# A fourth unscaled gate tile, a transposed copy of the S5 output, a column form of the last norm, and pools that wait tile by tile

## The chip, the cores and the metric

The kernel runs on one core of a Trainium2 chip. The metric is the device time of one execution in microseconds (us), as the median of three runs. The engines are named as in the profile: PE is TensorE's matmul, PEld its weight load, DVE is VectorE, ACT is ScalarE, POOL is GpSimd, and SP is the queue that issues most of the DMAs.

## What is computed

One layer of a hybrid decoder for T = 1056 tokens: 1024 of a prompt and 8 sequences of 4 sampled tokens, D = 1024 channels, all in float32.

```
h      = rmsnorm(x, g_mix)
q,k,v,u,gates = split(h @ w_in)            # 1024 | 256 | 256 | 1024 | 2048 columns
a_out  = attention(q, k, v) @ w_attn_o     # window 128, 16 heads, sinks
y      = S5(u)                             # diagonal state space, 64 groups of 16 channels
glu    = gelu(y) @ w_glu
s_out  = glu[:, :1024] * sigmoid(glu[:, 1024:])
x      = x + (sigmoid(gates[:, :1024])*a_out + sigmoid(gates[:, 1024:])*s_out) @ w_out
x      = x + square(relu(rmsnorm(x, g_ffn) @ w_up)) @ w_down
out    = rmsnorm(x, g_final)
```

The new keys and values and the S5 states are returned too.

## The kernel before, in words

Channels lie on the 128 partitions and tokens along the free dimension, so x is 8 tiles of 128 by 1056. A product in float32 is made of three matmuls on rounded halves (lines 117 to 119): weights and activations are each split into a high part (a cast on ACT) and a low part (a subtraction on DVE). A weight block is loaded by SP into `raw`, cast at line 91 and subtracted at line 92; `raw`, `whi` and `wlo` have two buffers each. An output tile of 128 columns of weights takes three chunks of 352 tokens, with 8 times 3 matmuls each, and three PSUM banks (`mm`) for the chunks.

**The start.** `start` (line 166) loads the 8 tiles of x, and makes `hh` (line 181, ACT) and `hl` (line 182, DVE). The same function squares each x on ACT (line 186) and adds the squares into `acc` on POOL (line 188, seven additions of 128 by 1056). `first_tiles` multiplies the first two gate tiles, g0 and g1, with k outermost: each k of them needs only that `hh[k]` and `hl[k]` are there. `token_norms` (line 191) then turns `acc` into the norm factor of each token with small matmuls (line 198), a square root with one Newton step (`rsqrt_newton`, line 155), and spreads the factors over the partitions with matmuls against the identity (line 207) into `rb`. The first `RAW` gate tiles are stored without that factor; it is multiplied in much later, ahead of the sigmoid.

**The order of the tiles.** `cols_in` (line 97) lists the 26 tiles of w_in that come ahead of k and q: g0 g1 g2 u0 u1 u2, then u, g and g+5 in turn, the last gates, and v0, v1. `tile_in` takes the next of the list. A u tile is scaled and transposed into the buffer `Up` by DVE (`u_evac`, line 430), and `Up` (one buffer) goes to DRAM. S5 parameters (`s5_params`, some 150 DVE operations on 64 or 32 columns) and tables (`s5_tables`, with two multiplications on POOL, lines 391 and 402) are made meanwhile. In the loop over m (line 697 on), each of the eight S5 blocks is `s5_x` (matmuls of line 649, then a chain over ACT and DVE up to `HB`, lines 651 to 670) and `s5_y` (matmuls of line 680 that read `HB`, then GELU, then a store to `ydram`). Tiles are put between the two by hand, so that PE has work while the chain runs: one tile and `s5_b` where m is in `SKIP`, two otherwise.

**The middle.** After the S5 part come the two k tiles, the q tiles, and attention, in which a generator (`filler`) hands matmuls of q and of the GLU to PE between the attention blocks. `glu_input` (line 977) loads a tile of `ydram`, whose tokens lie in S5 order (token within block, block), and brings it to token order while it splits it: ACT at line 985, DVE at line 986, each in one piece of 1024 columns with a stride and one of 32. The first GLU tile has k outermost and needs each k as it comes.

**The end.** `last_down` (line 1492) adds the last part of w_down in three token chunks: 512, 288 and 256 tokens. For each of the 8 output tiles DVE adds (line 1543), ACT squares and scales (1545, 1546), and the squares are summed (line 1548: on POOL in the first chunk, on DVE in the others). While a chunk runs, `finish` normalizes the one before: one matmul with a matrix of ones gives each partition all the token sums (line 1497), Newton's square root runs on 128 by 512 or 128 by 288 elements (lines 157 to 162), and 8 multiplications (line 1506: all on POOL for the first chunk, half of them for the second) give the output, which SP stores. The last chunk is finished by rows (`finish_rows`).

**Queues and pools.** Each engine works its instructions off in one order, which is not that of the code: the trace shows DVE running parameter operations of line 276 on ahead of `hl` of later k. Memory comes from pools that are opened and closed; a pool opened over memory of a closed one is by default held until all that used the old pool is done. Line numbers here and in the rows are those of the kernel before.

Of the kernel before, what the change touches and what calls it, by code (L numbers as in the profile page):

```python
# [45 lines left out]
def hybrid_kernel(tc, xt, cache_k, cache_v, h0, norms, w_in, sinks, w_attn_o, lam_re, lam_im, log_dt,  # L46
# [17 lines left out]
    def bank(pool=None):  # L64
        return new(psax, [P, 512], F32, "ax")
# [19 lines left out]
    def wblock(w, n, nk=KT, pool=wts):  # L85

        raw = new(wts, [P, KT, P], F32, "raw")
        nc.sync.dma_start(raw[:, :nk], w[n])
        hi = new(pool, [P, KT, P], F32R, "whi")
        lo = new(pool, [P, KT, P], F32R, "wlo")  # L90
        nc.scalar.copy(hi[:, :nk], raw[:, :nk])  # L91
        nc.vector.tensor_tensor(lo[:, :nk], raw[:, :nk], hi[:, :nk].bitcast(F32), op=ALU.subtract)  # L92
        return hi, lo


    CB = {"u": 12, "g": 20, "v": 10}
    cols_in = [("g", 0), ("g", 1), ("g", 2), ("u", 0), ("u", 1), ("u", 2)]
    cols_in += [t for i in range(3, 8) for t in (("u", i), ("g", i), ("g", i + 5))]
    cols_in += [("g", i) for i in (13, 14, 15)] + [("v", 0), ("v", 1)]
    loaded = []  # L100

# [8 lines left out]
    def gemm(*args, **kw):  # L110
        for _ in gemm_steps(*args, **kw):
            pass
# [48 lines left out]
        nc.vector.tensor_scalar(tmp2, tmp2, -0.5, 1.5, op0=ALU.mult, op1=ALU.add)  # L161
        nc.vector.tensor_tensor(out, tmp1, tmp2, op=ALU.mult)

    RAW = 3

    def start(st, small_loads):

        nc.scalar.dma_start(gcol, norms)
        acc = new(st, [P, T], F32, "acc")
        xs = []  # L170
        for k in range(KT):
            x = new(st, [P, T], F32, "x", 8)
            nc.sync.dma_start(x, xt[k])
            if k in (0, PF2):
                prefetch(wts if k else st)
            if k == PF3:
                prefetch()
            if k == SLK:
                small_loads()
            g = gcol[:, 0, k:k + 1]  # L180
            nc.scalar.activation(hh[k], x, AF.Copy, scale=g)
            nc.vector.scalar_tensor_tensor(hl[k], x, g, hh[k].bitcast(F32), op0=ALU.mult, op1=ALU.subtract)  # L182
            xs.append(x)
        for k, x in enumerate(xs):
            sq = new(st, [P, T], F32, "sq", 3) if k else acc
            nc.scalar.activation(sq, x, AF.Square)
            if k:
                (nc.vector if k in AV else nc.gpsimd).tensor_tensor(acc, acc, sq, op=ALU.add)
        return acc

    def token_norms(st, acc):
# [17 lines left out]
            nc.scalar.copy(rb[:, 3 * c * P:3 * c * P + w], ps[:, :w])  # L209

    PF3 = 5
    AV, PF2, SLK = (), 1, 1


    AR0, AI0, R8 = 0, 9, 18
# [169 lines left out]
    def s5_tables(Y, Ys, fr, fi):  # L385
        nc.scalar.activation(XC[64:128], XC[64:128], AF.Copy, scale=-1.0)
        nc.scalar.activation(Ys[0:64], Ys[0:64], AF.Copy, scale=-1.0)

        sh = [P, G, CH]
        nc.vector.tensor_tensor(BB, Y, fr[:, :, None].to_broadcast(sh), op=ALU.mult)  # L390
        nc.gpsimd.tensor_tensor(Ys, Ys, fi[:, :, None].to_broadcast(sh), op=ALU.mult)
        nc.vector.tensor_tensor(BB, BB, Ys, op=ALU.add)

        H0s = new(slabA, [P, 4, SB, 16], F32, "slab")
        swap(H0s, H0, s0=-1.0)
        sh = [P, 4, SB, 16]

        def pw(col):
            return TP[:, col].rearrange("p (q g) -> p q g", q=4)[:, :, None, :].to_broadcast(sh)

        nc.vector.tensor_tensor(FS, H0, pw(AR0 + 4), op=ALU.mult)
        nc.gpsimd.tensor_tensor(H0s, H0s, pw(AI0 + 4), op=ALU.mult)
        nc.vector.tensor_tensor(FS, FS, H0s, op=ALU.add)
    def s5_phases(TE):

# [113 lines left out]


    S5Q = nc.sync
    NT0 = 4
    with tc.tile_pool(name="ptmp", bufs=1) as pt:
        with tc.tile_pool(name="start", bufs=1) as st:
            prm = []
# [6 lines left out]
            tile_in()  # L532
        s5_tables(Y, Ys, *ft[:2])

    s5w = s5c.enter_context(tc.tile_pool(name="s5work", bufs=1))

    def s5_a(m):

# [187 lines left out]


    mid = es.enter_context(ExitStack())
    qpool = mid.enter_context(tc.tile_pool(name="qpool", bufs=4))
    gen = mid.enter_context(tc.tile_pool(name="gen", bufs=4))  # L730
    late = mid.enter_context(tc.tile_pool(name="late", bufs=1))
    WIN = 128
    kpool = es.enter_context(ExitStack())
    kp = kpool.enter_context(tc.tile_pool(name="kpool", bufs=2))
    kk = [new(kp, [P, T], F32, "kk") for _ in range(2)]

    def scaled_evac(dst, s=None):
        def ev(n, cs, ps):
            if s is None:
                nc.vector.tensor_tensor(dst[:, cs], ps, rb[:, cs], op=ALU.mult)  # L740
            else:
                nc.vector.scalar_tensor_tensor(dst[:, cs], ps, s, rb[:, cs], op0=ALU.mult, op1=ALU.mult)
        return ev

    for i in range(2):
        gemm(wblock(w_in, KT + i), hh, hl, 8, scaled_evac(kk[i]))
    for i in range(2):
        nc.gpsimd.dma_start(k_prompt[i], kk[i][:, SEQ - WIN:SEQ])

# [225 lines left out]
    sdram = [new(dram, [P, T], F32, f"sd{m}") for m in range(KT)]  # L975

    def glu_input(k):
        yt = new(gen, [P, TC, NY], F32, "slab")
        nc.sync.dma_start(yt, ydram[k])
        h = new(slabA, [P, T], F32R, "slab")  # L980
        l = new(slabA, [P, T], F32R, "slab")
        for o, i, pat in ((slice(0, SEQ), yt[:, :, 0:NK], "p (k j) -> p j k"),
                          (slice(SEQ, T), yt[:, 0:ST, NK:NY], "p (b j) -> p j b")):
            hv = h[:, o].rearrange(pat, j=i.shape[1])
            nc.scalar.copy(hv, i)
            nc.vector.tensor_tensor(l[:, o].rearrange(pat, j=i.shape[1]), i, hv.bitcast(F32), op=ALU.subtract)
        gh.append(h)
        gl.append(l)

# [35 lines left out]
        for _ in range(n):  # L1025
            next(fill, None)

    with tc.tile_pool(name="attn", bufs=1) as atp:
        prev = turned = None
        for m in range(2):  # L1030
            for _ in q_proj(m):
                pass
        units = [(kv, blk) for kv in range(NKV) for blk in range(NB)]
        qs = split_q(0, 0)
        kh = new(atp, [P, SEQ], F32R, "kh")
        kl = new(atp, [P, SEQ], F32R, "kl")
        key_stack(0, 0)
        for u, (kv, blk) in enumerate(units):
            if blk == 0:
                key_stack(kv, 1)  # L1040
            if blk == KAHEAD and kv + 1 < NKV:
                key_stack(kv + 1, 0)
            qs, qn = (split_q(*units[u + 1]) if u + 1 < len(units) else None), qs
            cur = (kv, blk) + attend_p(kv, blk, qn, kh, kl)
            more(MORE[u][0])
            if turned is not None:
                attend_v(*turned)
            turned = attend_t(*prev) if prev is not None else None
            more(MORE[u][1])
            prev = cur  # L1050
        attend_v(*turned)
        turned = attend_t(*prev)
        more(2)
        attend_v(*turned)
    with tc.tile_pool(name="sattn", bufs=1) as sp:
        qd = [new(sp, [P, SB, ST, NH], F32, "qd", 2) for _ in range(2)]
        smask = new(sp, [NR, NKEY], F32, "smask")
        vn4 = new(sp, [ST, SB, NKV * HD], F32, "vn4")
        sample_queries()
        prev = None  # L1060
        for g in range(SB // GB):
            if g % 2 == 0:
                load_cache(g // 2)
            cur = sample_p(g)
            more(SMORE[0])
            if prev is not None:
                sample_v(*prev)
            prev = cur
            more(SMORE[1])
        sample_v(*prev)  # L1070
# [421 lines left out]
    def last_down(ws, fh, fl):  # L1492

        def finish(c0, cw, acc):

            ps = bank()
            nc.tensor.matmul(ps[:, :cw], ones, acc[:, :cw], start=True, stop=True)
            ms = new(slabA, [P, 2, 512], F32, "slab")
            r = new(const, [P, T], F32, "rb")[:, :cw]
            nc.vector.tensor_scalar(ms[:, 0, :cw], ps[:, :cw], 1.0 / D, EPS, op0=ALU.mult, op1=ALU.add)  # L1500
            rsqrt_newton(r, ms[:, 0, :cw], acc[:, :cw], ms[:, 1, :cw])
            yield
            for m in range(KT):
                yo = new(slabB, [P, 512], F32, "slab")[:, :cw]
                e = nc.gpsimd if m in YP[c0 > 0] else nc.vector
                e.tensor_tensor(yo, x2[m][:, c0:c0 + cw], r, op=ALU.mult)
                o = min(c0, 512)
                nc.sync.dma_start(y_cols[m, :, o:o + cw], yo)
                yield

        def finish_rows(c0, tiles, acc, banks):

# [8 lines left out]
            for i, (t0, w) in enumerate(tiles):  # L1521
# [2 lines left out]
                nc.scalar.activation(yo[:, 512:], banks[i][1], AF.Copy, scale=r[:, i:i + 1])  # L1524
                for h, eng in enumerate((nc.sync, nc.scalar)):
                    eng.dma_start(y_rows[t0 - c0:t0 - c0 + w, h * 512:h * 512 + 512], yo[:, h * 512:h * 512 + 512])

        YP = (range(8), (1, 3, 5, 7))

        def turn(pss, k, t0, w):  # L1530
            nc.tensor.transpose(pss[k // 4][:w, (k % 4) * P:(k % 4 + 1) * P], x2[k][:, t0:t0 + w], ident)
# [119 lines left out]
```

## Time and profile before

| | us |
|---|---|
| runs (median of 3, lowest to highest) | 1719.57 (1718.57 to 1720.12) |
| the profiled execution, its own time | 1723.68 |
| its span, first to last instruction | 1720.6 |
| PE busy | 1652.6 (96%) |
| DVE busy | 1254.6 (73%) |
| ACT busy | 865.1 (50%) |
| POOL busy | 288.6 (17%) |
| mean granted PE clock | 0.982 of full speed |

The span is measured between instructions; some 3.1 us of the execution lie outside it. A granted clock of 1.0 is 2.4 GHz, 0.5 is 1.2 GHz. Busy times of PE overlap between neighbours, since matmuls are pipelined; what one of them takes is read from the distance of their starts.

### The profile page before, as it was taken

To read this page: it belongs to the slowest core of one execution; us is meant where nothing else is said; L and a number is where in the kernel's file an instruction comes from. 1 tells how busy PE (TensorE), PEld (TensorE's weight loads), DVE (VectorE), ACT (ScalarE), POOL (GpSimd) and SP (SyncE) were. 2 spreads that over 40 slices of the span, in tenths; PEclk is the share of its full clock that TensorE was granted. 3 is DMA by queue.
4 is the path that set the end of the run, shared out by engine and by line. 5 is a ranking of instruction groups with operands and counts; after the bars stand their busy time and mean duration, and the time that the engine had idled before them with its cause. 6 is when DMAs were issued, how large, how long until landed. Compare 5 with 4: busy or idle time off the path is not lost. (4 is left out here: it accounts for less than half of the span.)

```text
span 1720.6 us, 30881 instructions
## 1 busy us (share of the span) xinstructions
PE 1652.6 (96%) x11952; PEld 1618.7 (94%) x11952; DVE 1254.6 (73%) x2449; ACT 865.1 (50%) x1878; POOL 288.6 (17%) x250
## 2 busy tenths in 40 slices
PE   6989999999999899989999999999999999999997
PEld 5979999999999799979999999999999999999986
DVE  8888787744488999952543677777777788787857
ACT  5344444332267888854432555444444645454454
POOL 5211111101133443521122330000000000000014
PEclk8989999999999999999999999999999999999999
DMA  5144433443110321133343563444444665353322
GB/s 208 63 151 139 136 98 121 139 122 112 53 38 26 102 89 50 63 100 111 117 136 126 185 193 113 145 138 144 154 154 148 220 203 182 112 182 113 113 56 101
DMA packets 131685, 213.16 MB, mean 124 GB/s; under 512 B 13756, under 2 KB 86540, under 8 KB 131028
## 3 DMA queue, kind: packets, MB, share of 16 engines
q1 hardware_dynamic: 84452, 162.16, 29.6%
q10 hardware_dynamic: 45360, 46.63, 8.0%
q0 software_dynamic: 1728, 2.41, 0.6%
q8 instruction: 93, 1.52, 0.4%
q14 instruction: 52, 0.43, 0.1%
HBM read 146.26 MB, written 64.90 MB: 123 GB/s over the span
## 5 line engine op out<-in xcount | busy, mean ns | idle before, releaser
L118 PE MATMUL mm<-slab,whi 128*128 128x352 f32 (+3 forms) x1688 | 532.3, 316 | 20.8 <-DVE slab L182 12.6
L117 PE MATMUL mm<-slab,whi 128*128 128x352 f32 (+3 forms) x1688 | 537.2, 320 | 10.2 <-DVE Up L435 8.1
L119 PE MATMUL mm<-slab,wlo 128*128 128x352 f32 (+3 forms) x1688 | 531.7, 315 | 0.3 <-DVE wlo L92 0.3
L1240 PE MATMUL ax<-slab,w 128*128 128x264 f32 x3600 | 452.0, 285 | 2.6 <-DVE acc L1315 2.5
L1240 PEld LDWEIGHTS ax<-slab,w 128*128 128x128 f32 x3600 | 443.9, 188 | 4.0 <-DVE acc L1315 3.7
L118 PEld LDWEIGHTS mm<-slab,whi 128*128 128x128 f32 x1688 | 322.5, 191 | 24.4 <-DVE slab L182 13.6
L117 PEld LDWEIGHTS mm<-slab,whi 128*128 128x128 f32 x1688 | 320.5, 190 | 13.1 <-issue 9.7
L119 PEld LDWEIGHTS mm<-slab,wlo 128*128 128x128 f32 x1688 | 321.4, 190 | 0.8 <-DVE wlo L92 0.6
L1240 PE MATMUL mm<-slab,w 128*128 128x264 f32 x1440 | 186.7, 284 | 1.9 <-DVE w L1351 1.2
L1240 PEld LDWEIGHTS mm<-slab,w 128*128 128x128 f32 x1440 | 179.8, 188 | 2.5 <-DVE w L1351 1.4
L91 ACT CAST whi<-raw 128x1024 fp32r<-128x1024 f32 x76 | 79.6, 1047 | 101.5 <-PE mm L118 64.6
L1351 DVE TENSOR_TENSOR w<-raw,w 128x512 fp32r<-128x512 f32 (+2 forms) x96 | 63.0, 657 | 77.2 <-ACT w L1350 75.4
L1548 POOL TENSOR_TENSOR slab<-slab,slab 128x512 f32<-128x512 f32 x7 | 9.1, 1293 | 634.3 <-ACT slab L1545 634.3
L92 DVE TENSOR_TENSOR wlo<-raw,whi 128x1024 fp32r<-128x1024 f32 x76 | 100.1, 1318 | 17.9 <-ACT whi L91 17.5
L804 POOL TENSOR_TENSOR qs<-q,qs 64x256 fp32r<-64x256 f32 x64 | 62.1, 971 | 69.7 <-ACT qs L803 58.9
L1350 ACT CAST w<-whi 128x512 fp32r<-128x512 f32 (+2 forms) x64 | 38.0, 594 | 70.7 <-PE ax L1240 32.7
L828 ACT ACTIVATE pm<-pm,sm 128x128 f32<-128x128 f32 x128 | 49.9, 391 | 33.7 <-DVE sm L825 33.5
L1264 ACT ACTIVATE slab<-slab 128x264 f32<-128x264 f32 x80 | 33.9, 425 | 61.3 <-DVE slab L1263 44.1
L843 POOL TENSOR_TENSOR pt<-fb,pt 128x512 fp32r<-128x512 f32 x28 | 42.7, 1526 | 120.0 <-ACT pt L842 76.5
L1350 ACT CAST w<-raw 128x512 fp32r<-128x512 f32 (+2 forms) x96 | 56.8, 593 | 9.6 <-PE mm L1240 7.6
L568 POOL TENSOR_TENSOR tmp<-bbs,TP 128x1024 f32<-128x1024 f32 x8 | 20.6, 2576 | 206.5 <-DVE W L557 206.5
L1351 DVE TENSOR_TENSOR w<-wlo,w 128x512 fp32r<-128x512 f32 (+2 forms) x64 | 42.1, 658 | 5.4 <-ACT w L1350 4.4
(404 smaller groups left out, 2721.8 us busy)
## 6 DMA issues: line engine op xcount, KB each, us to landing
raw<-in_w_in_dram SPq DMA_DIRECT2D x36, 512.0 KB
raw<-in_w_up_dram SPq DMA_DIRECT2D x32, 512.0 KB
ffd<-slab ACTq DMA_DIRECT2D x28, 528.0 KB
gt<-ffd SPq DMA_DIRECT2D x53, 264.0 KB
slab<-ffd SPq DMA_DIRECT2D x53, 264.0 KB
raw<-in_w_down_dram SPq DMA_DIRECT2D x22, 512.0 KB
gd<-gt ACTq DMA_DIRECT2D x48, 176.0 KB
slab<-gd SPq DMA_DIRECT2D x16, 528.0 KB
```

The costliest lines, as they stand in the source:

```text
L91: nc.scalar.copy(hi[:, :nk], raw[:, :nk])
L92: nc.vector.tensor_tensor(lo[:, :nk], raw[:, :nk], hi[:, :nk].bitcast(F32), op=ALU.subtract)
L117: nc.tensor.matmul(ps[:, :cw], w[0][:, k, :], ah[k][:, cs], start=(k == 0), stop=False)
L118: nc.tensor.matmul(ps[:, :cw], w[0][:, k, :], al[k][:, cs], start=False, stop=False)
L119: nc.tensor.matmul(ps[:, :cw], w[1][:, k, :], ah[k][:, cs], start=False, stop=(k == nk - 1))
L804: nc.gpsimd.tensor_tensor(qs[b, :, h], q[a, :, bs], qs[a, :, h].bitcast(F32), op=ALU.subtract)
L828: nc.scalar.activation(pm[:, i], pm[:, i], AF.Exp, bias=ng[:, i:i + 1], accum_out=den[:, i:i + 1])
L843: lo(pt[:, 1], src, pt[:, 0].bitcast(F32), op=ALU.subtract)
L1240: nc.tensor.matmul(ps[:, :CQ], w[:, wp, js], b[:, bp], start=start and j == k == 0, stop=j == n - 1 and k == 2, skip_group_check=True)
L1264: nc.scalar.activation(dst, dst, AF.Square)
L1350: nc.scalar.copy(t[:, 0], s)
L1351: V.tensor_tensor(t[:, 1], s, t[:, 0].bitcast(F32), op=ALU.subtract)
```

## The change

- One more gate tile, g3, comes ahead of u0 and is stored without the norm factor (`RAW` 4, `NT0` 5); the list of tiles is shifted accordingly, so that the loop over m holds one tile fewer, and the last block has one tile between `s5_x` and `s5_y` in place of two.
- The seven additions of squares at the start and the two multiplications of `s5_tables` go from POOL to DVE.
- A new `turn_y` runs beside the two k tiles: it loads each tile of `ydram`, brings it to token order with two ACT copies, and stores it to `ynat`. `glu_input` loads `ynat` and splits it with one ACT and one DVE operation of 1056 contiguous columns.
- `finish` makes the norm factors in columns: small matmuls with one output column per 128 (or 96) tokens, Newton's step on 128 by 4 or 96 by 3 elements, matmuls against the identity that spread the factors into a PSUM bank, and 8 multiplications on DVE that read that bank. It hands on two outputs at a time.
- The pools of the S5 work, of the middle and of both attention parts wait tile by tile (`reuse_waits="tile"`): a tile waits only for those older tiles whose bytes it takes.

```diff
-    cols_in = [("g", 0), ("g", 1), ("g", 2), ("u", 0), ("u", 1), ("u", 2)]
-    cols_in += [t for i in range(3, 8) for t in (("u", i), ("g", i), ("g", i + 5))]
+    cols_in = [("g", 0), ("g", 1), ("g", 2), ("g", 3), ("u", 0), ("u", 1), ("u", 2), ("u", 3), ("g", 8)]
+    cols_in += [t for i in range(4, 8) for t in (("u", i), ("g", i), ("g", i + 5))]
...
-    RAW = 3
+    RAW = 4
...
-                (nc.vector if k in AV else nc.gpsimd).tensor_tensor(acc, acc, sq, op=ALU.add)
+                nc.vector.tensor_tensor(acc, acc, sq, op=ALU.add)
...
-        nc.gpsimd.tensor_tensor(Ys, Ys, fi[:, :, None].to_broadcast(sh), op=ALU.mult)
+        nc.vector.tensor_tensor(Ys, Ys, fi[:, :, None].to_broadcast(sh), op=ALU.mult)
...
-        nc.gpsimd.tensor_tensor(H0s, H0s, pw(AI0 + 4), op=ALU.mult)
+        nc.vector.tensor_tensor(H0s, H0s, pw(AI0 + 4), op=ALU.mult)
...
-    NT0 = 4
+    NT0 = 5
...
-    s5w = s5c.enter_context(tc.tile_pool(name="s5work", bufs=1))
+    s5w = s5c.enter_context(tc.tile_pool(name="s5work", bufs=1, reuse_waits="tile"))
...
+    ynat = [new(dram, [P, T], F32, f"yn{k}") for k in range(KT)]
+
+    def turn_y(k):
+
+        yt = new(gen, [P, TC, NY], F32, "slab")
+        nc.sync.dma_start(yt, ydram[k])
+        yn = new(gen, [P, T], F32, "slab")
+        for o, i, pat in ((slice(0, SEQ), yt[:, :, 0:NK], "p (k j) -> p j k"),
+                          (slice(SEQ, T), yt[:, 0:ST, NK:NY], "p (b j) -> p j b")):
+            nc.scalar.copy(yn[:, o].rearrange(pat, j=i.shape[1]), i)
+        nc.sync.dma_start(ynat[k], yn)
+
     for i in range(2):
         gemm(wblock(w_in, KT + i), hh, hl, 8, scaled_evac(kk[i]))
+        for k in range(4 * i, 4 * i + 4):
+            turn_y(k)
...
     def glu_input(k):
-        yt = new(gen, [P, TC, NY], F32, "slab")
-        nc.sync.dma_start(yt, ydram[k])
+        y = new(gen, [P, T], F32, "slab")
+        nc.sync.dma_start(y, ynat[k])
...
-            hv = h[:, o].rearrange(pat, j=i.shape[1])
-            nc.scalar.copy(hv, i)
-            nc.vector.tensor_tensor(l[:, o].rearrange(pat, j=i.shape[1]), i, hv.bitcast(F32), op=ALU.subtract)
+        nc.scalar.copy(h, y)
+        nc.vector.tensor_tensor(l, y, h.bitcast(F32), op=ALU.subtract)
...
         def finish(c0, cw, acc):
 
+            n = 96 if cw % P else P
+            nt = cw // n
+            ms, r, t1, t2 = (small4(nt, tag=t, bufs=1) for t in ("os", "or", "oa", "ob"))
             ps = bank()
-            nc.tensor.matmul(ps[:, :cw], ones, acc[:, :cw], start=True, stop=True)
...
-            rsqrt_newton(r, ms[:, 0, :cw], acc[:, :cw], ms[:, 1, :cw])
+            for i in range(nt):
+                nc.tensor.matmul(ps[:n, i:i + 1], acc[:, i * n:i * n + n], ones[:, 0:1], start=True, stop=True)
+            nc.vector.tensor_scalar(ms[:n], ps[:n, :nt], 1.0 / D, EPS, op0=ALU.mult, op1=ALU.add)
+            rsqrt_newton(r[:n], ms[:n], t1[:n], t2[:n])
             yield
+            ps = bank()
+            for i in range(nt):
+                nc.tensor.matmul(ps[:, i * n:i * n + n], r[:n, i:i + 1].to_broadcast([n, P]), ident[:n, :n],
+                                 start=True, stop=True)
             for m in range(KT):
                 yo = new(slabB, [P, 512], F32, "slab")[:, :cw]
-                e = nc.gpsimd if m in YP[c0 > 0] else nc.vector
-                e.tensor_tensor(yo, x2[m][:, c0:c0 + cw], r, op=ALU.mult)
+                nc.vector.tensor_tensor(yo, x2[m][:, c0:c0 + cw], ps[:, :cw], op=ALU.mult)
...
-                yield
+                if m % 2:
+                    yield
```

The pools `qpool`, `gen`, `late`, `kpool`, `attn` and `sattn` get `reuse_waits="tile"` in the same way as `s5work`.

## Rows read from the trace of the kernel before

**Rows 1.** The page's busy times, the row of PE.

```profile
PE 1652.6 (96%) x11952; PEld 1618.7 (94%) x11952; DVE 1254.6 (73%) x2449; ACT 865.1 (50%) x1878; POOL 288.6 (17%) x250
```

**Rows 2.** Waits of PE: who waited for whom, us in total, times, longest.

```profile
PE mm L118 <- DVE slab L182: 12.6, 2, 11.0
PE mm L117 <- DVE Up L435: 8.1, 1, 8.1
PE mm L118 <- DVE slab L986: 7.0, 7, 1.8
...
PE ax L680 <- DVE FP L670: 4.6, 3, 3.4
PE ax L1497 <- DVE slab L1548: 2.6, 1, 2.6
...
PE ax L920 <- POOL smask L909: 0.9, 1, 0.9
```

**Rows 3.** Windows: stretch, length, busy of five engines, PE clock, DMA share, GB/s.

```profile
0.00:50.00 50.00, 34.25 (x181) 32.72 (x181) 41.82 (x98) 24.41 (x25) 22.27 (x24) 0.83 0.49 186
...
8.29:15.70 7.41, 7.09 (x39) 6.20 (x39) 7.41 (x11) 7.41 (x8) 3.32 (x2) 1.00 0.92 363
...
98.50:112.78 14.28, 14.25 (x72) 14.28 (x73) 13.10 (x16) 2.07 (x5) 2.26 (x1) 0.79 0.66 212
...
410.00:455.00 45.00, 45.00 (x293) 44.80 (x292) 14.77 (x28) 9.12 (x17) 6.45 (x16) 1.00 0.36 112
554.00:585.00 31.00, 22.32 (x123) 19.44 (x122) 28.81 (x40) 29.10 (x45) 13.68 (x6) 0.96 0.40 124
...
1681.00:1712.50 31.50, 26.92 (x192) 25.23 (x191) 28.02 (x45) 14.47 (x33) 15.27 (x12) 0.95 0.26 96
```

**Rows 4.** Timeline of PE in the first 50 us: start, length, line.

```profile
26.71 0.66 PE L118 MATMUL mm<-slab,whi 128*128 128x352 f32 x1 [11.02 <-DVE slab L182]
...
48.97 0.33 PE L119 MATMUL ax<-slab,wlo 128*128 128x352 f32 x1
```

**Rows 5.** Timeline of DVE in the first 50 us, one kind of operation twice.

```profile
15.08 2.48 DVE L279 SCALAR_TENSOR_TENSOR er<-ek,ex 128x64 f32<-128x64 f32 x1
...
36.17 0.22 DVE L280 SCALAR_TENSOR_TENSOR er<-ek,er 128x64 f32<-128x64 f32 x1
```

**Rows 6.** Groups of POOL in the first 50 us: busy, mean ns.

```profile
L188 POOL TENSOR_TENSOR acc<-acc,sq 128x1056 f32<-128x1056 f32 x7 | 18.3, 2608 | 8.4 <-ACT sq L186 8.0
```

**Rows 7.** Timeline of DVE between 50 and 135 us, evacuation of u1.

```profile
97.64 1.36 DVE L435 TENSOR_TENSOR Up<-mm,rb 128x352 f32<-128x352 f32 x2
```

**Rows 8.** Timeline of PE, the start of the last `s5_x`.

```profile
383.61 2.01 PE L649 MATMUL ax<-U,W 128*128 128x136 f32 x16
```

**Rows 9.** Timeline of DVE, the end of the last chain (beside `HB`).

```profile
399.17 0.16 DVE L670 TENSOR_TENSOR FP<-T,xy 128x8 f32<-128x8 f32 x1
```

**Rows 10.** Groups of DVE and ACT from 540 to 590 us, shapes apart.

```profile
L986 DVE TENSOR_TENSOR slab<-slab,slab 128x1024 fp32r<-128x1024 f32 x8 | 17.4, 2173 | 1.0 <-ACT slab L985 1.0
L92 DVE TENSOR_TENSOR wlo<-raw,whi 128x1024 fp32r<-128x1024 f32 x2 | 2.4, 1210 | 0.0
...
L985 ACT CAST slab<-slab 128x1024 fp32r<-128x1024 f32 x8 | 17.1, 2142 | 0.0
...
L1000 ACT ACTIVATE slab<-slab 128x1056 f32<-128x1056 f32 x2 | 2.2, 1084 | 0.0
```

**Rows 11.** Groups of DVE from 1680 us on, shapes apart.

```profile
L1548 DVE TENSOR_TENSOR slab<-slab,slab 128x288 f32<-128x288 f32 x7 | 6.0, 862 | 0.8 <-ACT slab L1545 0.7
...
L1543 DVE TENSOR_TENSOR acc<-mm,acc 128x288 f32<-128x288 f32 x8 | 3.6, 447 | 2.3 <-PE mm L119 2.3
L158 DVE RECIPROCAL slab<-slab 128x512 f32<-128x512 f32 x1 | 3.4, 3354 | 0.3 <-ACT slab L157 0.3
```

**Rows 12.** Timeline of PE from 47 to 58 us, the small matmuls of `token_norms`.

```profile
49.13 1.99 PE L198 MATMUL ax<-ones,acc 128*128 128x1 f32 x18
...
54.89 2.28 PE L207 MATMUL ax<-ident,r 128*128 128x128 f32 x18
```

More of the change, by code (lines that the diff above doesn't have):

```diff
@@ L211, in hybrid_kernel @@
     PF3 = 5
-    AV, PF2, SLK = (), 1, 1
+    PF2, SLK = 1, 1
     AR0, AI0, R8 = 0, 9, 18
@@ L728, in hybrid_kernel @@
     mid = es.enter_context(ExitStack())
-    qpool = mid.enter_context(tc.tile_pool(name="qpool", bufs=4))
-    gen = mid.enter_context(tc.tile_pool(name="gen", bufs=4))
-    late = mid.enter_context(tc.tile_pool(name="late", bufs=1))
+    qpool = mid.enter_context(tc.tile_pool(name="qpool", bufs=4, reuse_waits="tile"))
+    gen = mid.enter_context(tc.tile_pool(name="gen", bufs=4, reuse_waits="tile"))
+    late = mid.enter_context(tc.tile_pool(name="late", bufs=1, reuse_waits="tile"))
     WIN = 128
     kpool = es.enter_context(ExitStack())
-    kp = kpool.enter_context(tc.tile_pool(name="kpool", bufs=2))
+    kp = kpool.enter_context(tc.tile_pool(name="kpool", bufs=2, reuse_waits="tile"))
     kk = [new(kp, [P, T], F32, "kk") for _ in range(2)]
@@ L977, in glu_input @@
     def glu_input(k):
-        yt = new(gen, [P, TC, NY], F32, "slab")
-        nc.sync.dma_start(yt, ydram[k])
+        y = new(gen, [P, T], F32, "slab")
+        nc.sync.dma_start(y, ynat[k])
         h = new(slabA, [P, T], F32R, "slab")
         l = new(slabA, [P, T], F32R, "slab")
-        for o, i, pat in ((slice(0, SEQ), yt[:, :, 0:NK], "p (k j) -> p j k"),
-                          (slice(SEQ, T), yt[:, 0:ST, NK:NY], "p (b j) -> p j b")):
-            hv = h[:, o].rearrange(pat, j=i.shape[1])
-            nc.scalar.copy(hv, i)
-            nc.vector.tensor_tensor(l[:, o].rearrange(pat, j=i.shape[1]), i, hv.bitcast(F32), op=ALU.subtract)
+        nc.scalar.copy(h, y)
+        nc.vector.tensor_tensor(l, y, h.bitcast(F32), op=ALU.subtract)
         gh.append(h)
@@ L1026, in more @@
             next(fill, None)
-    with tc.tile_pool(name="attn", bufs=1) as atp:
+    with tc.tile_pool(name="attn", bufs=1, reuse_waits="tile") as atp:
         prev = turned = None
@@ L1054, in hybrid_kernel @@
         attend_v(*turned)
-    with tc.tile_pool(name="sattn", bufs=1) as sp:
+    with tc.tile_pool(name="sattn", bufs=1, reuse_waits="tile") as sp:
         qd = [new(sp, [P, SB, ST, NH], F32, "qd", 2) for _ in range(2)]
@@ L1494, in finish @@
         def finish(c0, cw, acc):
+            n = 96 if cw % P else P
+            nt = cw // n
+            ms, r, t1, t2 = (small4(nt, tag=t, bufs=1) for t in ("os", "or", "oa", "ob"))
             ps = bank()
-            nc.tensor.matmul(ps[:, :cw], ones, acc[:, :cw], start=True, stop=True)
-            ms = new(slabA, [P, 2, 512], F32, "slab")
-            r = new(const, [P, T], F32, "rb")[:, :cw]
-            nc.vector.tensor_scalar(ms[:, 0, :cw], ps[:, :cw], 1.0 / D, EPS, op0=ALU.mult, op1=ALU.add)
-            rsqrt_newton(r, ms[:, 0, :cw], acc[:, :cw], ms[:, 1, :cw])
+            for i in range(nt):
+                nc.tensor.matmul(ps[:n, i:i + 1], acc[:, i * n:i * n + n], ones[:, 0:1], start=True, stop=True)
+            nc.vector.tensor_scalar(ms[:n], ps[:n, :nt], 1.0 / D, EPS, op0=ALU.mult, op1=ALU.add)
+            rsqrt_newton(r[:n], ms[:n], t1[:n], t2[:n])
             yield
+            ps = bank()
+            for i in range(nt):
+                nc.tensor.matmul(ps[:, i * n:i * n + n], r[:n, i:i + 1].to_broadcast([n, P]), ident[:n, :n],
+                                 start=True, stop=True)
             for m in range(KT):
                 yo = new(slabB, [P, 512], F32, "slab")[:, :cw]
-                e = nc.gpsimd if m in YP[c0 > 0] else nc.vector
-                e.tensor_tensor(yo, x2[m][:, c0:c0 + cw], r, op=ALU.mult)
+                nc.vector.tensor_tensor(yo, x2[m][:, c0:c0 + cw], ps[:, :cw], op=ALU.mult)
                 o = min(c0, 512)
                 nc.sync.dma_start(y_cols[m, :, o:o + cw], yo)
-                yield
+                if m % 2:
+                    yield
         def finish_rows(c0, tiles, acc, banks):
@@ L1526, in finish_rows @@
                     eng.dma_start(y_rows[t0 - c0:t0 - c0 + w, h * 512:h * 512 + 512], yo[:, h * 512:h * 512 + 512])
-        YP = (range(8), (1, 3, 5, 7))
         def turn(pss, k, t0, w):
```

## The prediction

> **What bounds the kernel now.** I read the page's busy times first, then the waits of PE, then windows over each stretch where PE waits, then the timelines of what it waits for. PE is busy for 96% of the span [rows 1], so only two things can be won: the 68 us in which PE idles, and the stretches in which its clock is granted at half speed. The waits say where [rows 2]. Four places carry the change. At the start PE waits for `hl` (line 182), 12.6 us in two pieces. Later it waits once, 8.1 us, for the evacuation of u1 into `Up` (line 435). While the GLU's first tile runs, it waits 7.0 us in seven pieces for the low parts of y (line 986). At the end it waits 2.6 us for a sum of squares (line 1548). After the first two long waits the clock costs more: behind the second, the 14.28 us of u2 run at a granted clock of 0.79 [rows 3], that is partly at 1.2 GHz, so 14.28 times 0.21 = 3.0 us are lost.
>
> **Start: squares added on DVE.** Why is `hl` late? It is one DVE operation per tile, but in the first 50 us DVE is busy for 41.82 [rows 3] with little work in it: an operation on 64 columns takes 2.48 us, and the same kind takes 0.22 once POOL is silent [rows 5]. POOL's seven additions take 2.6 us each [rows 6], the same length: each holds up one small DVE operation. With them gone, DVE wins about 7 times (2.48 - 0.22) = 15.8 us and gets 7 additions at 1.25 us each (1.21 us for 1024 columns [rows 10], times 1056/1024) = 8.7 us, and 1.8 us for the two multiplications of the tables (1024 and 512 columns at the same rate). Net: DVE is at least 5 us ahead. What is it worth to PE? PE stops at 26.71 - 11.02 = 15.7 us [rows 4] with 39 of the 144 matmuls of g0 and g1 done, as the window up to there counts [rows 3], and ends them at 49.1 [rows 4, 12]. The other 105 at 0.16 us, the distance from the last of them to the next instruction [rows 4, 12], would end at 32.5. The most to win is 16.6 us; that DVE must still do additions and `hl` side by side costs some. The other end is a gain of nothing. I take **-13**, nearest to the row of an undisturbed operation.
>
> A rule of the Trainium skill speaks against this step: "Perfetto Trace Analysis", section "Optimizing Scalar/DVE Operations", says that where DVE is saturated some work may go to Scalar or even GpSimd, though it warns that DVE and GpSimd share a port. By its first half, the move from POOL to a DVE busy for 84% of the stretch would cost time; rival (c) is what that would give. Rows 5 and 6 bear out the warning in place of the first half.
>
> **Fourth gate tile, and the wait for u1.** A g tile is 72 matmuls, 72 times 0.16 = 11.6 us. It is only moved ahead of u0, so its own matmuls cost nothing. Its evacuation moves from DVE to ACT, which is idle for half of the first 50 us [rows 3], and its factor is multiplied in later, in a stretch where PE has no wait of note; if that cover were gone, 1.25 us. PE would need u1's bank at 98.5 - 8.05 = 90.5 before; now at 90.5 - 13 + 11.6 = 89.1. DVE reached that evacuation at 97.64 [rows 7]; being 5 to 8 us ahead (the upper figure if the two table multiplications also slowed operations beside them) it now gets there at 90 to 92. So 1 to 3 us of the wait stay, and most of the half clock goes: 8.05 + 3.0 - 3 = **-8**. Bounds: nothing, and -11. What is late next is DVE's work for block 0 (`s5_e`), which has one more tile behind it than before.
>
> **The last S5 block** has one tile less between its two halves. Its chain runs from 383.61 [rows 8] to 399.3 [rows 9], 15.7 us; of these PE now has the 2.0 us of `s5_x` and one tile of 11.6 us. **+2**; between 0 (the transposes of a v tile cover some) and 3.4, the longest such wait of a block with one tile between [rows 2].
>
> **Turning y early.** Eight loads of 0.56 MB (128 by 1088 floats), sixteen ACT copies and eight stores go beside the k and q tiles. There ACT is busy for 9.12 of 45 us, and the DMA moves 112 GB/s [rows 3], against 186 at the start. The copies are ACT's at line 985, 2.14 us [rows 10], some 19 us in all, and fit into the idle 36. Behind the waits for them stand the weight casts on ACT and the weight loads on SP, which run one tile ahead. **+0.5**; bounds 0 and the 20 of a rival below.
>
> **GLU input.** Each of the eight pieces now costs DVE 1.25 in place of 2.17 plus a small one, and ACT 1.08 in place of 2.14 [rows 10]. From 554 to 585 us DVE is busy for 28.81 of 31 us, ACT for 29.10, and PE idles for 8.7 [rows 3]. The work taken off is 8 times 0.92 = 7.4 us of DVE and 8.5 us of ACT, as long as PE's idle time. The half clock there is 0.04 times 31 = 1.2. **-7**; bounds 0 and -9.9.
>
> **The end.** From 1681 to 1712.5 us PE idles for 31.5 - 26.9 = 4.6 us and loses 0.05 times 31.5 = 1.6 us to the clock [rows 3]. DVE is the cause: a reciprocal of 3.35 us, and additions of 0.86 us beside POOL's multiplications, where an addition of the same shape alone takes 0.45 [rows 11]. The column form takes off both reciprocals and Newton's wide steps; it adds eight multiplications of about 0.7 and four more of 0.45, read from PSUM as line 1543 does [rows 11]. DVE has less to do in all. PE pays: an instruction of line 198 is 1.99/18 = 0.11 us, of line 207 2.28/18 = 0.13 [rows 12], two of each for 128 tokens, so 4 times 0.48 + 3 times 0.48 = 3.4 us in place of two matmuls of 0.9: +1.6. The spread also waits for a square root and five small steps, with one tile of PE work between; some +1 for both. -4.6 - 1.6 + 1.6 + 1 = -3.6, say **-3.5**; bounds -4.6 (no wait for the spread) and +2 (the old waits come back and the matmuls are extra).
>
> **Pools that wait tile by tile** free some first tiles earlier. The one wait of PE behind a freshly opened pool is 0.9 (line 920) [rows 2]. I take 0; at best -0.9. Nothing is read in the rows that it could make worse.
>
> **Sum:** -13 - 8 + 2 + 0.5 - 7 - 3.5 = -29. The profiled execution took 1723.7, so 1694.7; it lies 4.1 above the median of the runs, so 1690.6, and I say **1691**.
>
> **The rivals.**
> (a) DVE stays the limit of the first 110 us: the additions stand ahead of `hl`, or u1's evacuation moves less than I count. Then the start gives 6 and the second wait 2: 1691 + 13 = 1704. For it speaks that DVE is busy for 41.82 of the first 50 us [rows 3]; against it, that POOL's hold was the larger part. 20%.
> (b) The turn of y is not hidden: SP works load, copy and store off one after the other, and the weights stand behind. A load at 186 GB/s [rows 3] is 3.0 us, copies 2.4, a store 2.9; eight times 8.3 = 66 us, against four tiles of 46 us beside it: +20, 1711. Against it: the idle time of ACT and the low DMA rate there [rows 3]. 8%.
> (c) Slower: the small operations were not held up by POOL. Then DVE gets 8.7 + 1.8 = 10.5 us on top in the first stretch, both waits stay and the clock costs another 3.0, while the rest still gives -8: 1719.6 + 13.5 - 8 = 1725. It decides once DVE's first stretch grows by more than those 8. Rows 5 and 6 speak against it. 6%.
> (d) The change does not do what it says: the order on the queues shifts so that what is won at one wait is waited at the next, 1719.6. 4%.
>
> **How the numbers follow.** 62% for the forecast. The low end takes all terms at their better bound: -16.6 - 11 - 9.9 - 4.6 - 0.9 = -43, so 1677. The high end is (b), 1711, and takes (a) in. Outside lie (c), (d) and the tails, about 18%. A measurement of this kernel tells some 0.2% (3.4 us) from no change. Faster by more: 0.62 + 0.20 + 0.08, less 0.02 for their tails, 0.88. Within: 0.05. Slower: 0.07.
>
> **What the new profile would show.** Right: no POOL in the first 50 us but memsets and small things, DVE's small operations at 0.2 us throughout, the last matmul of the first two tiles near 36 us in place of 49, a wait at line 435 of under 3 us; in the GLU's first tile no waits of over 1 us; at the end no reciprocal over 0.3 us and PE idle for under 2 us. Wrong: small DVE operations of 2 us with POOL silent; a wait of PE for `hl` that has additions ahead of it in DVE's order; waits of PE for `whi` beside the k tiles; waits at line 680 of over 4 us.

## The result, and the profile after

The changed kernel took 1698.25 us (median of 4 runs, 1694.52 to 1702.79) where the kernel before took 1719.17 beside it: a ratio of 0.9879, 95% interval 0.9854 to 0.9904. That is 20.9 us faster; the forecast was 28.6. The profiled execution took 1699.22, its span is 1697.4, 23.2 less than before. In the line numbers of after, the GLU's low parts are line 997, the sums of squares at the end line 1563, and the column norm lines 1512 to 1522.

The windows over the stretches of [rows 3] (first 50 us; the tile behind u1's wait; the GLU's first tile; the end), same columns:

```profile
0.00:50.00 50.00, 46.93 (x289) 45.63 (x290) 41.00 (x132) 30.84 (x38) 5.06 (x17) 1.00 0.57 218
91.80:106.20 14.40, 14.40 (x73) 14.40 (x74) 14.33 (x17) 4.60 (x9) 3.02 (x1) 0.79 0.70 210
543.00:574.00 31.00, 28.98 (x175) 26.61 (x174) 30.73 (x47) 28.30 (x55) 13.52 (x8) 1.00 0.39 124
1658.50:1690.00 31.50, 30.22 (x241) 29.34 (x239) 23.05 (x63) 16.12 (x37) 1.97 (x2) 1.00 0.29 105
```

The waits of PE, against [rows 2]:

```profile
PE ax L460 <- DVE gt L484: 7.9, 1, 7.9
PE mm L117 <- DVE Up L435: 6.7, 1, 6.7
PE ax L680 <- DVE FP L670: 5.9, 4, 2.6
...
PE mm L118 <- DVE slab L997: 1.9, 4, 0.6
```

The wait for `hl` is gone and PE is busy for 46.93 of the first 50 us in place of 34.25. Two lines of DVE's timeline there show why, one of the seven additions and the operation of line 279 of [rows 5]:

```profile
12.49 1.25 DVE L188 TENSOR_TENSOR acc<-acc,sq 128x1056 f32<-128x1056 f32 x1
...
13.90 0.22 DVE L279 SCALAR_TENSOR_TENSOR er<-ek,ex 128x64 f32<-128x64 f32 x1
```

That operation took 2.48 us beside POOL's additions and takes 0.22 now. The GLU's seven pieces of waiting went from 7.0 to 1.9, and the wait for the end's sum of squares went. Two large waits are left: the one for u1, shorter by only 1.4 where under 3 us had been forecast, and a new one of 7.9 at line 460, the transposes of v.

Where the 23.2 us between the two spans come from can be read from PE's own milestones: the moment at which it has done so many tiles (72 matmuls of lines 117 to 119 each), against the same count before.

| PE has done | before, us | after, us | this stretch won | forecast |
|---|---|---|---|---|
| 2 tiles (start) | 49.1 | 32.6 | -16.5 | -13 |
| 7 tiles (wait for u1) | 124.6 | 106.2 | -1.9 | -8 |
| 28 tiles (S5 loop, v, k) | 438.6 | 426.7 | +6.5 | +2 |
| 36 tiles (q; turn of y beside k and q) | 556.6 | 544.7 | 0 | +0.5 |
| 37 tiles (GLU's first) | 584.6 | 563.9 | -8.8 | -7 |
| 46 tiles (attention) | 738.2 | 716.8 | -0.7 | 0 |
| 52 tiles (samples' attention) | 841.8 | 823.4 | +3.0 | 0 |
| end of the span | 1720.6 | 1697.4 | -4.8 | -3.5 |

The +3.0 of the samples' attention is the clock: over 130 us around it the granted clock was 0.92, against 0.95 before, with PE busy for 124.4 us in both. It is not tied to the change: in the traces of runs 4, 9, 10 and 11 below the clock there is 0.95 and the stretch takes as long as before.

The timelines of PE, of DVE and of POOL around the two waits that are left:

```profile
91.78 0.63 PE L117 MATMUL mm<-slab,whi 128*128 128x352 f32 x1 [6.67 <-DVE Up L435]
...
396.00 0.87 PE L460 MATMUL ax<-ident,gt 128*128 128x128 f32 x3 [7.88 <-DVE gt L484]
```

```profile
81.98 2.31 DVE L422 TENSOR_TENSOR slab<-slab,slab 128x64 f32<-128x64 f32 x1
84.81 2.62 DVE L421 TENSOR_TENSOR slab<-slab,slab 128x128 f32<-128x128 f32 x1
...
90.89 1.35 DVE L435 TENSOR_TENSOR Up<-mm,rb 128x352 f32<-128x352 f32 x2
...
388.74 1.21 DVE L669 TENSOR_TENSOR HB<-T,xy 128x1016 f32<-128x1016 f32 x1
...
395.30 1.02 DVE L484 TENSOR_TENSOR gt<-mm,rb 128x384 f32<-128x384 f32 x2 [3.15 <-DMA out_v_prompt_dram<-gt]
```

```profile
81.93 2.27 POOL L556 TENSOR_TENSOR tmp<-xc,TP 128x1152 f32<-128x1152 f32 x1 [2.44 <-DVE tmp L569]
84.67 2.61 POOL L568 TENSOR_TENSOR tmp<-bbs,TP 128x1024 f32<-128x1024 f32 x1 [0.47 <-DMA raw<-in_w_in_dram]
```

DVE came to u1 at 90.89, inside the forecast's 90 to 92, but PE had been waiting since 85.1. And what holds DVE is the same thing as at the start: an operation on 64 columns takes 2.31 us beside a POOL product of 2.27. At 396, v1's evacuation stands behind the chain of the last S5 block (its `HB` ends at 389.95) and then behind a DMA: the two `gt` buffers serve v's evacuation and v's float copies alike, and the copies leave by DMA.

### The profile page after: what moved, and what is told of

Same layout as the page of the kernel before. It is cut to its first block, busy times and chain, and to the rows that moved or that the text cites. A ratio compares the mean times of both kernels' runs of the same rounds, so it can differ in the third digit from the quotient of the medians.

```text
span 1697.4 us, 30950 instructions
## 1 busy us (share of the span) xinstructions
PE 1648.3 (97%) x11976; PEld 1617.2 (95%) x11976; DVE 1233.5 (73%) x2460; ACT 875.7 (52%) x1889; POOL 247.1 (15%) x229
## 5 line engine op out<-in xcount | busy, mean ns | idle before, releaser
L818 POOL TENSOR_TENSOR qs<-q,qs 64x256 fp32r<-64x256 f32 x64 | 58.2, 910 | 62.4 <-ACT qs L817 49.5
```

Source lines behind the costliest of these rows:

```text
L818: nc.gpsimd.tensor_tensor(qs[b, :, h], q[a, :, bs], qs[a, :, h].bitcast(F32), op=ALU.subtract)
```

## The experiments

Ratios are against the kernel before, run beside each group of them, with medians of 1720.5 to 1723.3 us.

**1. The squares back on POOL, all else changed.**

```diff
-                nc.vector.tensor_tensor(acc, acc, sq, op=ALU.add)
+                nc.gpsimd.tensor_tensor(acc, acc, sq, op=ALU.add)
```

> The changed kernel with only the seven additions of squares put back on POOL. Theory (one limit): POOL's additions hold up DVE's small operations, and DVE's arrival at the evacuation of u1 is what sets the pace of the first 92 us; so the first two tiles end near 49 us in place of 32.6, but the later wait at line 435 nearly vanishes, and u2 ends only 5 to 8 us later than the 106 us of the changed kernel: total +5 to +8, about 1704. Rival (two waits that add): the wait at line 435 stays at 6 to 7 us, and the total is 16 us later, about 1715. Second rival (POOL does not hold up DVE): small DVE operations stay at 0.2 us and the first tiles end near 33 us.

Measured: 1713.34 us, ratio 0.9958 (0.9943 to 0.9972), 15 us slower than the changed kernel. Its wait and its first window are those of before:

```profile
PE mm L118 <- DVE slab L182: 12.4, 2, 8.4
```

```profile
0.00:50.00 50.00, 34.70 (x181) 33.16 (x181) 41.64 (x98) 24.55 (x25) 22.25 (x24) 0.83 0.48 186
```

So one line carries most of the gain. The rival came out, that the two waits add: PE still waits 7.0 us for u (3.8 at line 435 and 3.2 at line 440, in five pieces). PE ends its first two tiles when it did before, and at tile 7 it is 4.3 us ahead, which is what the fourth gate tile wins without the faster start.

**2. That line alone, in the kernel before.**

```diff
-                (nc.vector if k in AV else nc.gpsimd).tensor_tensor(acc, acc, sq, op=ALU.add)
+                nc.vector.tensor_tensor(acc, acc, sq, op=ALU.add)
```

> The kernel before with only the additions of squares moved to DVE. Theory (one limit): the first two tiles end near 33 us in place of 49, but without the fourth gate tile ahead of u0 the wait at line 435 grows from 8 to 16 or 17 us, u2 ends near 106 in place of 112.9, and the total gains 5 to 8 us, about 1713. Rival (waits that add): the wait at line 435 stays near 8 us and the total gains 16 us, about 1703.

Measured: 1706.0 us, ratio 0.9911 (0.9876 to 0.9945).

```profile
PE mm L117 <- DVE Up L435: 10.6, 2, 7.6
```

PE ends the first two tiles at 32.4, 16.7 us earlier, as early as in the changed kernel. Only 2.5 of that comes back as more waiting for u than in [rows 2], and at tile 7 PE is still 13.4 us ahead. The two waits are nearly two sums, not one limit.

**3. v behind the last `s5_x`.** Block 3 gives its second tile to the last block, so that v0 no longer stands ahead of the last chain.

```diff
-    SKIP = (2, 4, 5, 6)
+    SKIP = (2, 3, 4, 5, 6)
```

> The changed kernel with block 3 added to SKIP, so that one tile moves from block 3 to the end, and both v tiles run behind the last s5_x, as in the kernel before. Theory: the 7.9 us wait of PE at line 460 comes from v0 standing ahead of the last chain: its last pieces wait in DVE's and ACT's order behind that chain, and v1 finds no free buffer. So that wait falls below 2 us, the half clock behind it goes (2 to 3 us), and block 3 may wait up to 2.6 us at line 680: total -6 to -10 against the changed kernel, about 1690. Rival: the wait is for the last HB itself, since only one tile covers it; then two tiles behind it take away 2 to 3 us at most, about 1696. Rival: v waits for its stores alone (the third piece of each v tile and its DMA); then the wait stays at 6 to 8 us, 1698 to 1700.

Measured: 1700.67 us, ratio 0.9883 (0.9856 to 0.991): nothing won. The wait at line 460 fell to 0.8, but the waits for the chains went up from 5.9 to 14.1:

```profile
PE ax L680 <- DVE FP L670: 10.2, 4, 3.4
...
PE ax L680 <- DVE HB L669: 3.9, 1, 3.9
```

The tile was not spare in block 3.

**4. The old order of the tiles.**

```diff
-    cols_in = [("g", 0), ("g", 1), ("g", 2), ("g", 3), ("u", 0), ("u", 1), ("u", 2), ("u", 3), ("g", 8)]
-    cols_in += [t for i in range(4, 8) for t in (("u", i), ("g", i), ("g", i + 5))]
+    cols_in = [("g", 0), ("g", 1), ("g", 2), ("u", 0), ("u", 1), ("u", 2)]
+    cols_in += [t for i in range(3, 8) for t in (("u", i), ("g", i), ("g", i + 5))]
...
-    RAW = 4
+    RAW = 3
...
-    NT0 = 5
+    NT0 = 4
```

> The changed kernel with the old list of tiles (three gate tiles ahead of u0, RAW 3, NT0 4). Theory: DVE reaches u1's evacuation at 91 us as in the changed kernel, so the wait at line 435 grows from 6.7 to 17 or 18 us and u2 ends again near 106 us with one tile less done (+11.6); at the end of the S5 part the wait of 7.9 us at line 460 and its half clock go (-8 to -11). Total within 4 us of the changed kernel, 1696 to 1702. Rival: the fourth gate tile brings nothing at the start, the wait at line 435 stays near 7 us, and the total is 8 to 11 us better, about 1688.

Measured: 1693.68 us, ratio 0.9839 (0.9808 to 0.9871), some 5 us faster than the changed kernel; these are two executions and the intervals overlap, but the traces show 4.0 us of it at tile 28. The wait for u is 8.3 us in two pieces, where the theory said 17 and the rival 7:

```profile
PE mm L117 <- DVE Up L435: 8.3, 2, 5.4
```

By tile 7 this kernel is 13.9 us ahead of before, the changed one 18.4: the fourth gate tile does win 4.5 there. By tile 28 it is 16.0 ahead, the changed one 12.0: without the fourth tile the wait at line 460 is 0.8. The shifted list gives back more than the tile wins.

**5. The old final norm** (`finish` of before, and its `YP`, as in the diff of the change).

> The changed kernel with the final norm of before (wide matmuls with ones, Newton's steps on whole columns, POOL multiplying half of the tiles). Theory, the end's gain is its own: the 4.2 us that the stretch from the last chunk of the output to the end of the span lost come back, so 1698.25 + 4.2 = 1702.5 us, ratio 0.990, with a reciprocal of 3.3 us and a wait of PE for the sum of squares of 2.6 us in the trace. Rival, those 4 us are a matter of how the half-speed stretches fell in the last 40 us and not of the norm: 1698 to 1699, ratio 0.988.

Measured: 1704.45 us, ratio 0.99 (0.9882 to 0.9918), 6 us slower (3.6 by the ratios). The reciprocal is back in the groups of DVE, and so is the wait:

```profile
L158 DVE RECIPROCAL slab<-slab 128x512 f32<-128x512 f32 x1 | 3.4, 3352 | 0.3 <-ACT slab L157 0.3
```

```profile
PE ax L1508 <- DVE slab L1559: 2.6, 1, 2.6
```

Most of that time goes near the end of the span. The window that corresponds to the last one of the result:

```profile
1667.00:1698.50 31.50, 26.49 (x182) 24.93 (x180) 26.68 (x44) 13.32 (x30) 15.27 (x12) 0.89 0.28 104
```

PE is busy for 26.49 us at a clock of 0.89, against 30.22 at 1.00 in the changed kernel. By the ratios the column norm is worth about the 3.5 us that were forecast, though the two intervals overlap; this window, of the slowest of the five executions, shows more.

**6. The old GLU input, no turn of y** (`glu_input` of before, the two lines that call `turn_y` taken out).

> The changed kernel with the GLU input of before and no turning of y ahead of time. Theory, the turn is free and the GLU's first tile alone paid: tiles 28 to 36 stand as in the changed kernel, tile 37 loses its 8.8 us, with some seven waits of PE for the low parts of y (7.0 us in all): 1698.25 + 8.8 = 1707 us, ratio 0.993. Rival, the turn costs the k and q tiles something that other gains cover: those tiles get 2 to 4 us shorter and the time is 1703 to 1705. Second rival, a GLU tile that ends earlier waits later in attention: 1698 to 1700, ratio 0.988.

Measured: 1704.93 us, ratio 0.9909 (0.9894 to 0.9925), 6.7 us slower. PE's waits for the low parts:

```profile
PE mm L118 <- DVE slab L998: 5.0, 4, 1.8
```

From tile 28 to tile 37 it took 7.6 us longer than the changed kernel. The k and q tiles alone (28 to 36) took 118.0 us without the turn and 118.0 with it, so there the turn cost nothing, and the whole difference lies in the GLU's first tile. The spans say less than these stretches here: ahead of tile 28, which the edit leaves alone, this execution was 2.9 us later than the changed kernel's, and its samples' attention took 99.0 us in place of 106.7, at a granted clock of 0.98 in place of 0.90.

**7. The pools as before** (`reuse_waits="tile"` taken out of all seven).

> The changed kernel with its seven pools waiting as before (no tile-wise waits). Theory, that part is worth nothing measurable, at best 0.9 us: 1698.3 to 1699.2 us, ratio 0.988, the waits of PE as in the changed kernel. Rival, the 3 us that the sample attention lost against before come from these pools: its stretch gets 3 us shorter, 1695.3 us, ratio 0.986.

Measured: 1700.83 us (1694.0 to 1704.21), ratio 0.9883 (0.9863 to 0.9903): no difference. The samples' attention was as long as in the changed kernel; its loss is not the pools'.

**8. The two POOL products of `s5_a` on DVE**, for blocks 0 and 1.

```diff
-        gp, V = nc.gpsimd, nc.vector
+        gp, V = nc.vector if m < 2 else nc.gpsimd, nc.vector
```

> The changed kernel with the two POOL products of the S5 weight tables of blocks 0 and 1 on DVE (four instructions of 1.2 to 1.35 us). Theory, what keeps DVE late for u1 is again POOL holding it: in the changed kernel four DVE instructions between 60 and 88 us took 2.29, 3.20, 2.31 and 2.62 us in place of some 0.2, 1.2, 0.25 and 0.3, so 8.4 us go and 5.1 come; the wait for u1 of 6.7 us falls to 3 or less and some of the half clock behind it goes too: 1692 to 1695 us, ratio 0.984 to 0.986. Rival, DVE simply has too much work there (58.7 of 60 us busy): 5.1 us more of it make the wait 11 to 12 us, and the time 1703, ratio 0.991.

Measured: 1693.61 us, ratio 0.9837 (0.9818 to 0.9857). With more work, DVE is earlier. In its timeline the operations of lines 422 and 421 that took 2.31 and 2.62 us beside POOL take 0.22 and 0.28, and u1's evacuation stands 6.5 us ahead of the changed kernel's; PE waits 2.5 for u in place of 6.7:

```profile
81.31 0.22 DVE L422 TENSOR_TENSOR slab<-slab,slab 128x64 f32<-128x64 f32 x1
...
82.06 0.28 DVE L421 TENSOR_TENSOR slab<-slab,slab 128x128 f32<-128x128 f32 x1
...
84.42 1.40 DVE L435 TENSOR_TENSOR Up<-mm,rb 128x352 f32<-128x352 f32 x2 [1.26 <-PE ax L579]
```

```profile
PE mm L117 <- DVE Up L435: 2.5, 1, 2.5
```

At tile 8 PE is 6.4 us ahead of the changed kernel, at tile 16 only 2.9: among others, a wait for block 2's chain that is now 2.96 us in place of 2.09, with a lower clock behind it, takes back the rest. In the changed kernel DVE was busy for 58.7 of the 60 us from 50 on. The Trainium skill ("Perfetto Trace Analysis", section "Optimizing Scalar/DVE Operations") says that where DVE is saturated, offloading some work to Scalar or even GpSimd may make sense; here the opposite won. The page's own warning, that GpSimd and DVE share a port, so that moves between these two might not help, is the half that agrees with these runs; they show how long DVE's operations take beside POOL's, not the port.

**9. Buffers of their own for v's float copies.**

```diff
-                    v32 = new(wts, [P, 384], F32, "gt")
+                    v32 = new(s5w, [P, P], F32, "v32", 2)
```

> The changed kernel with a pair of buffers of its own for the float copies of v, which shared the two buffers of the evacuations of g and v. Theory, the new wait of 7.9 us behind v1 is in part a buffer that a DMA out of the copies holds (DVE waited 3.15 us for it): that part goes, the wait falls to some 4.5 us and the time by 3 to 4: 1694.5 to 1695.5 us, ratio 0.9857. Rival, the chain of the last S5 block, which stands ahead of v1's evacuation on DVE, sets all of it: the wait stays over 7 us, time 1698, ratio 0.988.

Measured: 1690.91 us, ratio 0.9825 (0.9811 to 0.9838). The wait at line 460 falls to 0.5 us, not to 4.5: freed of the buffers, v1's first two evacuations stand between the operations of the chain on DVE. The second of them, where the changed kernel has both at 395.30:

```profile
384.67 0.56 DVE L484 TENSOR_TENSOR gt<-mm,rb 128x384 f32<-128x384 f32 x1 [0.56 <-PE mm L119]
```

The windows from 388 to 404 us, changed kernel and this one:

```profile
388.00:404.00 16.00, 8.12 (x46) 7.84 (x46) 7.98 (x23) 4.64 (x14) 5.64 (x14) 0.68 0.18 55
```

```profile
388.00:404.00 16.00, 15.54 (x108) 15.26 (x107) 9.18 (x26) 5.96 (x16) 7.17 (x17) 1.00 0.43 139
```

Tile 28 ends 10.4 us earlier than in the changed kernel, 22.4 ahead of before, but 5.4 of that lead are lost by tile 31, at a new wait and a lower clock behind it. Timelines of PE, ACT and SP's queue:

```profile
452.94 0.63 PE L853 MATMUL ax<-ident,pm 128*128 128x128 f32 x4 [3.11 <-ACT qs L817]
```

```profile
444.03 2.30 ACT L754 COPY slab<-slab 128x1024 f32<-128x1024 f32 x2 [3.84 <-DMA slab<-yd]
...
447.07 0.83 ACT L817 CAST qs<-q 64x256 fp32r<-64x256 f32 x2
```

```profile
435.23 0.42 SPq L88 DMA_DIRECT2D raw<-in_w_in_dram  x1
438.93 0.32 SPq L755 DMA_DIRECT2D yn<-slab  x1
439.34 0.38 SPq L750 DMA_DIRECT2D slab<-yd  x1
```

The last load of y stands on SP behind the store of the tile before, which waits for ACT's copies; its own copies stand on ACT ahead of `qs`, which the first attention blocks need.

**10. The turn off SP's queue as well.**

```diff
-        nc.sync.dma_start(yt, ydram[k])
+        nc.gpsimd.dma_start(yt, ydram[k])
...
-        nc.sync.dma_start(ynat[k], yn)
+        nc.scalar.dma_start(ynat[k], yn)
```

> The kernel with its own buffers for v's copies, and beside that the turning of y off SP's queue: its loads on POOL's queue, its stores on ACT's. In the trace of the own-buffer kernel the wait behind v1 went altogether (tile 28 ended 22.1 us earlier than before, against 12.0 in the changed kernel), but 6.4 us of that were lost again by tile 31, at a wait of 3.1 us for ACT's `qs`, which stands behind the last copies of y; SP held those copies' loads behind weight loads, in pairs some 11 us apart. Theory, that order on SP is the cause: the wait at line 853 goes, tile 31 ends 21 to 22 us ahead of before, and the time falls by 5 to 6 us, to 1685 to 1686, ratio 0.979 to 0.980. Rival, ACT's copies themselves or the DMA engines set it: the wait stays over 2 us and the time at 1690 to 1691, ratio 0.9825.

Measured: 1687.24 us, ratio 0.9807 (0.9787 to 0.9827). PE's wait for `qs` went; from tile 28 to 31 nearly nothing is lost (16.2 ahead, then 15.9). That the lead is 16 and not 22 comes mostly from the S5 blocks: against run 9, this trace loses 0.8 us at the start, 3.7 from tile 12 to 16, at a granted clock of 0.95 in place of 1.00, and 1.7 from tile 20 to 24, at 0.95 in place of 0.97. The last section tells of the larger one.

**11. Runs 8 and 10 together.**

> The kernel of the run before with the two weight-table products of blocks 0 and 1 on DVE as well. Theory, the gains add: their kernel alone was 2.8 us ahead of the changed one at tile 28 and stayed so: 1682 to 1684 us, ratio 0.978. Rival, a PE that comes earlier to the S5 blocks only waits longer for their chains (6.4 us ahead at tile 8 had shrunk to 2.8 by tile 16 in that kernel) and for y's turn: 1685 to 1687, no better than without.

Measured: 1681.4 us (1674.19 to 1687.17), ratio 0.9766 (0.974 to 0.9792): 39 us faster than the kernel before and some 17 faster than the changed one; against run 10 it is 5.8 us, with intervals that just overlap. No wait for u of over 0.6 us is left, and the two largest waits are for the chains and in attention:

```profile
PE ax L680 <- DVE FP L670: 6.6, 4, 2.8
PE ax L881 <- DVE pa L857: 5.0, 5, 1.9
```

**12. The same with the old order of the tiles** (the diff of run 4 on run 11).

> The kernel of the run before (1681.4 us) with the tile order of before: three gate tiles ahead of u0, two raw ones fewer among them, the tables after four tiles. Theory, the fourth gate tile is worth its 4.5 us at tile 7, as between the changed kernel and the one with the old order, and nothing takes that back now that v's copies have their own buffers: 1685 to 1687 us, ratio 0.979 to 0.980, with a wait for u1 of over 3 us. Rival, with POOL's products gone DVE is in time for u1 with three tiles too, or the S5 chains take back what PE wins ahead of them: 1680 to 1683 us, ratio 0.9766.

Measured: 1693.3 us (1687.15 to 1693.97), ratio 0.9829 (0.9813 to 0.9844), 12 us slower than run 11 (11 by the ratios). So the fourth gate tile pays once nothing gives it back. The reverse holds too: against run 4, which has this order without the edits of runs 8 to 10, the medians show nothing won (ratios of 0.9829 and 0.9839), so, as far as the medians tell, those edits paid only together with the fourth tile. PE's wait is now ahead of u1, for the tables of block 0:

```profile
79.28 1.97 PE L579 MATMUL ax<-ident,tmp 128*128 128x128 f32 x8 [7.34 <-DVE tmp L569]
```

The two traces show 4.3 us of the 12 (tile 28 ends 19.0 ahead of before, run 11's 23.3 ahead). The profiled executions took 1687.15 and 1685.15, at opposite ends of their runs; where the others lost the rest is open.

## Why the prediction was right, and where it was not

The kernel became faster and lies in the range, largely by the mechanisms named; the gain was put some 8 us too high. That the sum came so near is in part luck: by the milestones the start, the GLU and the end won 6.6 us more than their terms, and three other stretches won 13.6 us less.

- **Start, -13 against -16.5.** Right, and nearer to the better bound: additions and `hl` side by side cost almost nothing. Runs 1 and 2 show that the line of the additions does it: -16.7 alone. In this stretch small operations of DVE run at 0.2 us again, and rival (c) fell.
- **Fourth gate tile, -8 against -1.9.** The step that failed is "1 to 3 us of the wait stay". DVE's arrival (90 to 92) was right; PE's was not: it needed the bank at 85.1, not at 89.1, since the start had won 3.5 more than was put in. The half clock behind the wait stayed, 0.79 as before. Both terms together, -21, were measured as -18.4. The runs part the two: the tile itself is worth 4.3 (run 1 against before) or 4.5 (the changed kernel against run 4) at this place and not 8, and some 2.5 of what the start won were waited here (the changed kernel against run 1). Nor is DVE's arrival a fixed time that only PE's is set against: with the late start of run 1, u1's evacuation begins at 102.50 where the changed kernel has 90.89, and PE's wait there is 0.4 us. Rival (a) was half right, that DVE limits this stretch; the reason was not the additions but POOL's products, which run 8 shows.
- **The last S5 block, +2 against +6.5.** The mechanism was wrong. PE does not wait at line 680 for this block's chain. The tile that was moved ahead of it was v0, and v1 then could not be evacuated: two `gt` buffers shared with the float copies. Run 9 shows that it was the buffers; the chain alone did not hold PE, and from tile 7 to 28 that kernel won 3.6 where the changed one lost 6.5.
- **Turning y, +0.5 against 0.** Right (run 6), as long as PE comes to attention no earlier. Run 9 shows rival (b) in small: 10 us earlier, the turn was late.
- **GLU input, -7 against -8.8**, and **the end, -3.5 against -4.8**: right in kind; taken back singly they cost 5 to 7 us (run 6) and 4 to 6 us (run 5), the lower figures by the ratios. For the end that is not clear of noise.
- **Pools, 0**: right (run 7).
- The +3.0 of the samples' attention had no term. It is a granted clock lower by 0.03, in a stretch where the change touches only the pools, which run 7 clears.

## What to carry to other kernels

Two waits on the same engine are neither one limit nor two gains that simply add: of some 16.6 us won at the start, the next wait took back 2.5 with four gate tiles ahead of it and 3.3 with three. Work out the second as the arrivals of the one that waits and of the one waited for, and let a run with only one of the two changes price each. Where the list of tiles is shifted, look at which tile lands where, and at every buffer that this tile shares: here it was not the tile that was missing but the v tile in its place. And ask of each POOL operation beside a busy DVE what DVE does meanwhile: the time for which it is held counts as busy, so a DVE that was 98% busy had room for more. Moving the additions to DVE was a clear gain (runs 1 and 2), moving the products was one by the medians (runs 8 and 11); with the old order of the tiles (run 12) PE then waits 7.3 us for those very tables on DVE.

## What was not expected of the hardware

The clock makes a wait cost more than itself, and not evenly. Block 2's chain made PE wait 1.96 us in run 9 and 2.77 in run 10, with the same code there. The windows from 217 to 232 us of run 9 and of run 10:

```profile
217.00:232.00 15.00, 13.04 (x94) 12.96 (x90) 10.90 (x13) 9.01 (x19) 4.80 (x2) 1.00 0.52 150
```

```profile
217.00:232.00 15.00, 12.22 (x80) 11.82 (x79) 9.96 (x11) 6.90 (x13) 1.60 (x1) 0.77 0.43 123
```

At a granted clock of 0.77 in place of 1.00, 15 times 0.23 = 3.5 us were lost behind a wait that was 0.8 longer. In run 10 the clock is 1.00 up to 218 us, PE then waits until 220.7, and from 221 to 224 us the clock is 0.50. Executions of one kernel lay 7 to 13 us apart in runs 10 to 12; that such stretches make that spread is argued, not shown.
